# Row factors spread over partitions on TensorE, a longer allowance for transfers in the planner, and two staging buffers for output weights

## The chip, the cores and the metric

One core of a Trainium2 chip runs the kernel. The metric is the device time of one execution in microseconds (us), lower is better; the time of the kernel before is the median of three runs. A profile is one further execution with the hardware profiler on. The engines are called PE (TensorE), DVE (VectorE), ACT (ScalarE), POOL (GpSimd) and SP (SyncE, which issues all the DMAs of this kernel). Each engine runs its own list of instructions in order.

## What is computed

One encoder layer on a sequence of 4096 tokens with 1024 features, all float32 in and out:

```python
h = rmsnorm(x, pre_norm_g)
q, k, v, g_a, u_p, g_p = jnp.split(h @ w_in, splits, axis=-1)
a = banded_attention(q, k, v, rel_bias, sink) * jax.nn.silu(g_a)
p = multiscale_pool(u_p, pool_w, pool_scale) * jax.nn.silu(g_p)
mixed = jnp.concatenate([a, p], axis=-1) @ w_out
x = x + rmsnorm(mixed, post_norm_g)
```

`rmsnorm` multiplies each token by one number, its row factor: one over the root of the mean of the squares of its 1024 features. The attention looks 128 tokens to both sides; the pooling takes means over windows of 2, 4, 8 and 16 tokens.

## The kernel before, in words

Products are made of float16 pairs (a high part and the rest), three matmuls in place of one, and as blocks of 2 by 2 with seven products in place of eight. The program has two parts, one behind the other on every engine.

**Part A** (up to about 540 us) makes the three 512-wide projections: gate of the pooling `g_p` (GP), pooled values `u_p` (UU) and gate of the attention `g_a` (GA). The tokens come in 8 chunks of 512, `m` = 0 to 7. Chunk 0 is multiplied plainly (`plain`, tiles `plain`); chunks 1 to 7 have three `quad`s each, one for GP, UU and GA. A quad has seven products of 24 matmuls of 128x256 on the PSUM banks `y` (two of them, by turns), `x` and `v`. The first two, into `y` and `x`, read `xb`, the chunk's operands; the third reads `xt`, the sums of them; four of the seven read `xt`. Between the first and the third, ACT copies the bank (`keep`, line 718, `cc<-y`), since the third adds to it.

**What makes a chunk ready** is `prepare(m)`. Four times it loads 128 tokens into the one tile `xn` and ACT squares and sums them (`square`, line 324); POOL then takes the power, which leaves 512 row factors in `rs4`, token by partition (`root`). The operands, though, have features on partitions and tokens along the row, so the factors are needed along the row, the same in every partition. For that, SP stores `rs4` into memory (`rs_store`, line 907) and loads it back, spread over 128 partitions, into `rsb` (`rs_load`, line 910). For each of four slices `c`, DVE then multiplies the transposed tokens `nt` by gain and factor (`norm`, line 309, `nt<-nt,gsc,rsb`, two of 128x512), ACT makes the high parts of `xb` and DVE the rest, DVE makes the sums, and ACT and DVE split these into `xt`. For chunk 0 alone the factors are spread by PE already: DVE multiplies an identity by the factors of 128 tokens, a column of them at a time (`diag`), and a matmul of all ones with that diagonal leaves each factor in all partitions (`spread`, line 384).

**The order of part A comes from a planner** (`Steps`). Every step is given with its engine, an estimate of its time, a rank (`key`) and the names that it reads and writes. `run` plays the steps on five engines: the engine that is free soonest takes, of the steps whose inputs are ready by then, the one of the lowest rank. The order that comes out is the order of the program, fixed before it runs; on the chip, semaphores make each instruction wait for its data. A transfer is taken to move one after the other at the given length, and to be readable 1.8 us after its end:

```python
if dma:
    dma_free = max(dma_free, t + us) + dma
    end = dma_free + 1.8
```

SP's steps stand in one list too: a store that waits for its data holds every load behind it.

**Also in part A**: at chunk 0 `u_prod` multiplies the weights of UU by `pool_w` on PE, ACT squares the result and DVE copies it (`u_keep`, line 868). At chunks 1 to 3 the weights of q, k and v are split (`wb_steps`), and at chunks 5 and 6 those of the output (`wo_steps`): for each of four slices, four times `wo_keep` has ACT cast a weight tile into `RAW[:, 3]`, DVE make the rest beside it, and SP store both with two DMAs.

**Part B** (from line 1159 on) is the attention and the output projection. Its order is a list of its own, by written times; the change doesn't touch it.

Of the kernel before, what the change touches and what calls it, by code (L numbers as in the profile page):

```python
# [8 lines left out]
F32 = mybir.dt.float32  # L9
# [4 lines left out]
ALU = mybir.AluOpType  # L14
# [42 lines left out]
class Steps:  # L57
# [28 lines left out]
    def run(self):  # L86
        n_steps = len(self.steps)
        users = [[] for _ in range(n_steps)]
        open_deps = []
        for n, s in enumerate(self.steps):  # L90
            open_deps.append(len(s[5]))
            for d in s[5]:
                users[d].append(n)
        ready = [0.0] * n_steps
        begun = [None] * n_steps
        free = dict.fromkeys(("PE", "DVE", "ACT", "POOL", "SP"), 0.0)
        dma_free = 0.0
        waiting = {e: [] for e in free}
        for n in range(n_steps):
            if not open_deps[n]:  # L100
                waiting[self.steps[n][0]].append(n)
        left = n_steps
        while left:
            best = None
            for e, ns in waiting.items():
                if ns:
                    t = max(free[e], min(ready[n] for n in ns))
                    if best is None or t < best[0]:
                        best = (t, e)
# [12 lines left out]
            left -= 1  # L122
            for u in users[n]:
                ready[u] = max(ready[u], end)
                open_deps[u] -= 1
                if not open_deps[u]:
                    waiting[self.steps[u][0]].append(u)
        self.begun, self.end = begun, max(free.values())
        for n in sorted(range(n_steps), key=lambda n: (begun[n], n)):
            _, _, _, fn, args, _, _ = self.steps[n]  # L130
            fn(*args)
# [3 lines left out]
def hybrid_layer(ctx: ExitStack, tc, io, out):  # L135
# [41 lines left out]
    f_scr = dram.tile([NH, FR + 1, NF], F32, name="f_scr")  # L177
    rs_scr = dram.tile([NM, T], F32, name="rs_scr")
    x_scr = dram.tile([NU, P, 2, 2, 2, HK, P], F16, name="x_scr")
# [30 lines left out]
    with ExitStack() as actx:  # L210
# [18 lines left out]
        diags = [pa.tile([P, P], F32, name=f"diag{i}") for i in range(2)]  # L229
# [150 lines left out]
        def diag(i):  # L380
            t_scalar(V, diags[i // 2], ident, rs4[:, i : i + 1], ALU.mult)

        def spread(i):
            nc.tensor.matmul(
                bc[0][:, i * P : (i + 1) * P], onesf, diags[i // 2], start=True, stop=True,
                skip_group_check=True,
            )

# [74 lines left out]
        for h in range(2):  # L463
# [16 lines left out]
            for i in blocks:  # L480
                do("DVE", 0.25, -3, diag, i, r=["ident", f"rs{h}"], w=[f"diag{i // 2}"])
                do("PE", 0.5, -3, spread, i, r=["onesf", f"diag{i // 2}", "bc"], w=[f"bc{i}"])
            for c in range(HK):
# [216 lines left out]
        def quad(m, q, g):  # L700
# [48 lines left out]

            xbk_ = xkeys(m, "b")  # L750
            xtk = xkeys(m, "t")
            prod(0, yb, y, Y, A11, x_b(m, 0, 0), xbk_, True, False)
# [93 lines left out]

        ld(9, pw, io["pool_w"].rearrange("j p c -> p j c"), 0.25, w=["pw"])
        wut = flat32(XT0).rearrange("p (j c) -> p j c", j=4)
# [24 lines left out]
        for j in range(4):  # L873
            ld(9.5 + 0.1 * j, wut[:, j], io["w_uT"][j], 0.5, w=[f"wut{j}"])
            z = turn("sq")
            for half in range(2):
                t = U0 + 4 * j + 2 * half
                do("PE", 1.0, t, u_prod, j, half, r=["pw", f"wut{j}"], w=[f"wup{half}"] + bcs)
                do("ACT", act(512), t + 1.2, u_square, j, half, z, r=[f"wup{half}"], w=[f"sqt{z}"])
                do("DVE", dve(512), t + 1.2, u_keep, j, half, r=[f"sqt{z}"],  # L880
                   w=[f"wup{half}", f"tile{UU}.{j}{half}"])
            do("PE", 0.5, U0 + 4 * j + 5, w_norm, z, "u4", j, 4, b, r=["ones", f"sqt{z}"],
               w=[f"n2{b}"])
# [21 lines left out]

        def rs_store(m):
            nc.sync.dma_start(rs_scr[m].rearrange("(i p) -> p i", p=P), rs4)

        def rs_load(m):
            nc.sync.dma_start(  # L910
                rsb, rs_scr[m].rearrange("(o t) -> o t", o=1).to_broadcast([P, T])
            )

        def prepare(m):
            key = start(m) - 55
            b = m % 2
            for i in range(4):
# [3 lines left out]
               w=["rs4", "rs0", "rs1"])  # L921
            do("SP", 0.45, key + 4, rs_store, m, r=["rs4"], w=["rsd"], dma=0.1)
            do("SP", 0.45, key + 5, rs_load, m, r=["rsd"], w=["rsb", "pw"], dma=0.8)
            for c in range(HK):
# [4 lines left out]
                for h in range(2):  # L929
                    do("DVE", dve(512), k + h, norm, m, c, h, r=["gs", "rsb"], w=[n])  # L930
                x_operands(m, c, k + 2, "DVE")
# [34 lines left out]
        def row_prod():  # L966
            row_t["p"] = psa.tile([NH, 512], F32, name="fp", tag="wup0")
            nc.tensor.matmul(row_t["p"], row_t["b"], row_t["o"], start=True, stop=True)
# [14 lines left out]
        def row_steps(key):  # L983
            do("SP", 0.9, key, row_load, w=["row", "sqt0"], dma=0.3)
            do("PE", 1.8, key + 5, row_prod, r=["row", "sqt0"], w=["rowp", "wup0"])
            do("DVE", 0.7, key + 8, row_keep, r=["rowp", "wup0"], w=["rows", "sqt1"])
            do("SP", 0.45, key + 10, row_store, r=["rows", "sqt1"], w=["frow"], dma=0.1)
# [94 lines left out]

        stage16 = RAW[:, 3].bitcast(F16).rearrange("p (v c) -> p v c", v=2)

# [5 lines left out]

        def wo_store(k, o):
            for i in range(2):
                nc.sync.dma_start(w_scr[o + i, :, :, k, :], stage16[:, :, i * 512 : i * 512 + 512])

        def wo_keep(k, i, o, key):
            do("ACT", act(D), key, lambda: A.copy(stage16[:, 0], RAW[:, i]), r=[f"RAW{i}"],
               w=["RAW3"])
            do("DVE", dve(D), key + 1,
               lambda: tt(V, stage16[:, 1], RAW[:, i], stage16[:, 0], ALU.subtract),
               r=[f"RAW{i}"], w=["RAW3"])  # L1100
            do("SP", 0.9, key + 2, wo_store, k, o, r=["RAW3"], dma=1.8)

        def wo_steps(k, key):
# [5 lines left out]
            do("ACT", act(D), key + 1, wo_scale, 1, HK + k, r=["rowsc"], w=["RAW1"])  # L1109
            wo_keep(k, 0, O11, key + 2)  # L1110
# [4 lines left out]
            wo_keep(k, 1, O21, key + 8)  # L1115
            wo_keep(k, 2, OT1, key + 14)
# [4 lines left out]
            wo_keep(k, 0, OT4, key + 20)  # L1121

# [6 lines left out]
        for m in range(1, NM):  # L1129
# [820 lines left out]
```

## Time and profile before

| | |
|---|---|
| time, median of 3 runs | 1226.35 us (1225.23 to 1227.17) |
| the profiled execution | 1232.08 us; its span, first to last instruction, 1230.2 us |
| granted TensorE clock, mean | 0.991 |
| PE matmul busy | 1158.8 us, 94% |
| DVE, ACT, POOL busy | 952.0, 695.5 and 321.6 us (77%, 57%, 26%) |
| DMA moved | 227.92 MB |

In a row of the timeline stand the start and the duration in us, engine, line, operation and tiles (out<-in, with shapes), and the count of instructions that were joined; in brackets the time for which the engine had been idle before, and what ended that. Buffer numbers are left out: `y` is a bank of any quad. In the table by stretches stand, for each stretch, its length, then for PE, PEld (weight loads), DVE, ACT and POOL the busy time and the count, then the granted clock, the share of the DMA engines and GB/s. SPq is SP's list of DMAs; a row there is an issue, not the transfer.

### The profile page before, as it was taken

The page shows a single profiled execution, that of the slowest core. Times are in us where ns is not written, and L with a number is a line of the kernel's source. Part 1 is how long each engine was busy: PE and PEld are TensorE (multiplying, and loading weights), DVE is VectorE, ACT ScalarE, POOL GpSimd, SP SyncE. Part 2 cuts the span into 40 slices and gives each one's busy share as a digit, 9 for nine tenths or more (in the row PEclk, how much of TensorE's full clock was granted, in tenths as well). Part 3 has the DMA queues.
Part 4 walks back from the last instruction along what each step waited for, and adds up shares of the span by engine and source line. Part 5 has one row for each costly group of instructions (what it writes and reads, how often), then busy time and mean ns, then how long its engine had stood idle before and what let it go on. Part 6 is the DMA issues. An engine that isn't in the chain of part 4 may idle for free. (4 is left out here: it accounts for less than half of the span.)

```text
span 1230.2 us, 31539 instructions
## 1 busy us (share of the span) xinstructions
PE 1158.8 (94%) x13153; PEld 886.2 (72%) x13158; DVE 952.0 (77%) x1876; ACT 695.5 (57%) x1435; POOL 321.6 (26%) x310
## 2 busy tenths in 40 slices
PE   4995978999999999999999999999999999999997
PEld 4984867888888888886666776767676666767643
DVE  7868868797878978356778778777887887787786
ACT  5754545462635544236666756666576567566662
POOL 1002111112010202011254344434433533443331
PEclk9997998999999999999999999999999999999999
DMA  9635478966857555377989767866776786677694
GB/s 325 222 102 176 119 173 278 222 223 183 288 122 247 162 158 191 112 248 156 242 171 206 158 140 193 201 163 156 198 184 132 190 206 167 130 197 155 145 251 120
DMA packets 306848, 227.92 MB, mean 185 GB/s; under 512 B 205921, under 2 KB 269665, under 8 KB 302097
## 3 DMA queue, kind: packets, MB, share of 16 engines
q1 hardware_dynamic: 306704, 225.90, 69.9%
q8 instruction: 103, 1.69, 0.6%
q14 instruction: 41, 0.33, 0.1%
HBM read 116.78 MB, written 60.34 MB: 144 GB/s over the span
## 5 line engine op out<-in xcount | busy, mean ns | idle before, releaser
L604 PEld LDWEIGHTS <-wq 128*128 128x128 f16 x4104 | 404.3, 99 | 91.1 <-issue 34.3
L604 PE MATMUL y<-xt,wq 128*128 128x256 f16 x1512 | 179.2, 276 | 18.5 <-ACT cc L718 18.4
L1277 ACT ACTIVATE p<-p,nm 128x385 f32<-128x385 f32 (+1 forms) x256 | 153.0, 599 | 59.1 <-POOL p L1260 37.9
L1198 PE MATMUL aq<-xb,xb 128*128 128x256 f16 x1024 | 173.0, 273 | 4.5 <-DVE mo L1550 4.4
L1307 DVE SCALAR_TENSOR_TENSOR pn<-p,rd,pn 128x384 f16<-128x384 f32 (+1 forms) x256 | 156.5, 658 | 26.3 <-ACT pn L1299 26.3
L1522 PE MATMUL ms<-wo,ys 128*128 128x512 f16 x720 | 162.7, 379 | 1.8 <-ACT pn L1299 1.8
L1266 DVE CUSTOM_DVE_ANT_0 p<-s,nt,nsink 128x384 f32<-128x384 f32 (+1 forms) x256 | 156.0, 665 | 1.3 <-PE s L1243 1.1
L1299 ACT ACTIVATE pn<-p,rd 128x384 f16<-128x384 f32 (+1 forms) x256 | 136.3, 596 | 23.9 <-ACT p L1277 21.1
L1198 PEld LDWEIGHTS <-xb 128*128 128x128 f16 x1280 | 125.0, 98 | 22.8 <-issue 6.5
L1198 PE MATMUL aq<-xb,xt 128*128 128x256 f16 x512 | 139.5, 273 | 0.0
L1522 PEld LDWEIGHTS <-ys 128*128 128x128 f16 x720 | 69.0, 98 | 83.7 <-issue 3.0
L306 POOL TENSOR_TENSOR yt<-yt,sg 128x512 f32<-128x512 f32 (+2 forms) x32 | 50.7, 1586 | 290.6 <-DVE yt L309 246.6
L1522 PE MATMUL m<-wo,y 128*128 128x512 f16 x540 | 119.7, 379 | 1.4 <-POOL y L1427 0.7
L1522 PEld LDWEIGHTS <-y 128*128 128x128 f16 x540 | 51.4, 98 | 64.9 <-issue 3.6
L1556 POOL TENSOR_TENSOR mo<-mo,gpost 128x512 f32<-128x512 f32 x39 | 64.5, 1655 | 85.3 <-ACT jkb L1545 84.1
L1284 DVE TENSOR_SCALAR den<-den 128x4 f32<-128x4 f32 x64 | 17.4, 272 | 76.6 <-ACT p L1277 76.5
L604 PE MATMUL plain<-xb,wq 128*128 128x256 f16 x576 | 68.4, 277 | 5.3 <-ACT wq L537 2.5
L1388 PE MATMUL o<-pt,vv 128*64 128x256 f16 x1128 | 68.7, 274 | 3.6 <-DMA pt<-pn 3.6
L1198 PEld LDWEIGHTS <-xt 128*128 128x128 f16 x640 | 62.6, 98 | 12.6 <-issue 4.1
L604 PE MATMUL y<-xb,wq 128*128 128x256 f16 x504 | 60.7, 278 | 7.6 <-DVE ubuf L298 7.5
L1388 PEld LDWEIGHTS <-vv 128*64 128x64 f16 x1128 | 59.2, 110 | 10.4 <-issue 9.0
L1243 PE MATMUL s<-k_all,q 64*32 64x288 f16 (+7 forms) x3648 | 63.0, 266 | 3.1 <-ACT q L1186 1.4
(194 smaller groups left out, 1899.5 us busy)
## 6 DMA issues: line engine op xcount, KB each, us to landing
xn<-in_x SPq DMA_DIRECT2D x28, 512.0 KB, 3.9
nt<-in_xT SPq DMA_DIRECT2D x28, 512.0 KB, 5.3
x_scr<-xb SPq DMA_DIRECT2D x14, 1024.0 KB, 9.9
xb<-x_scr SPq DMA_DIRECT2D x14, 1024.0 KB, 7.8
xr<-in_x SPq DMA_DIRECT2D x28, 512.0 KB, 4.6
out<-xr SPq DMA_DIRECT2D x28, 512.0 KB, 3.7
ga_scr<-cc SPq DMA_DIRECT2D x64, 128.0 KB, 2.4
raw<-in_w_out SPq DMA_DIRECT2D x16, 512.0 KB, 8.0
```

What stands on the lines that cost most here:

```text
L306: eng.tensor_tensor(out=out, in0=in0, in1=in1, op=op)
L604: nc.tensor.matmul(b[:, s].rearrange("p (u t) -> p u t", u=2), wq[:, slot[q, op], wv, s, k, :], x[:, :, xv, k, :], start=(first and k + s ...
L1198: nc.tensor.matmul(a3, w[:, j, k, :], x[:, :, kh, v, kt, :], start=(n == 0), stop=(n == 3 * KT - 1),)
L1243: nc.tensor.matmul(s_ps[qs, gg, c0:c1], q_t[u, half][a, qi, jj, tl + 32 * hq : tl + 32 * hq + 32], k_all[a, ki, kc + c0 - s0 : kc + c1 - s ...
L1266: nc.vector.tensor_tensor_reduce(out=p_t[b, half][:, hh, :nk], in0=s_t[jj][:, gg, :nk], in1=bias[:, h, lo : lo + nk], scale=negc[:, h : h ...
L1277: nc.scalar.activation(p[:, hh, : nk + 1], p[:, hh, : nk + 1], AF.Exp, bias=nm_t[b, half][:, hh : hh + 1], scale=-1.0, accum_out=den_t[b, ...
L1284: nc.vector.tensor_scalar(out=den, in0=den, scalar1=1.0 / P_SCALE, scalar2=None, op0=ALU.mult)
L1299: nc.scalar.activation(prob_view(b, half)[:, 0, i], p_t[b, half][:, i, :nk], AF.Copy, scale=rd_t[b, half][:, i : i + 1],)
L1307: nc.vector.scalar_tensor_tensor(out=pn4[:, 1, i], in0=p_t[b, half][:, i, :nk], scalar=rd_t[b, half][:, i : i + 1], in1=pn4[:, 0, i], op0= ...
L1388: nc.tensor.matmul(o_ps[a, 2 * half : 2 * half + 2], v[:, vi, kt, a], pt[b, half][:, pi, g, :, i, :], start=(n == 0), stop=(n == last),)
L1522: nc.tensor.matmul(z_t[u, tag], y[:, k, yi, :], wo[o][:, wi, k, :], start=(n == 0 and acc is None), stop=(n == 3 * HK - 1), skip_group_che ...
L1556: eng.tensor_tensor(out=mo, in0=mo, in1=gpost[:, cs], op=ALU.mult)
```

## The change

1. **Row factors.** For chunks 1 to 7, DVE multiplies the identity by all 512 factors at once into a diagonal `dg` of 128 x 4 x 128 (`diag_all`), one matmul of 128x512 with the ones spreads them into a PSUM bank (`spread_all`), and `norm` reads that bank in place of `rsb`. The store and the load through memory go. The bank has a tag of the two that `u_prod` used (`wup0`, `wup1`), by turns; the small product of the bias rows moves from that tag to `n20`. `pool_w` now lies in the tile `ws`.
2. **Planner.** From 25 us on, what a transfer brings is readable 5.0 us after its end, not 1.8. So steps are put in another order on all engines; no transfer is changed by that itself.
3. **Planner, products.** Each product of a quad becomes four steps of six matmuls, each waiting only for its slice of the operands. The matmuls are the same, but the planner may now put pieces of two or three products in turn.
4. **`u_keep`** moves from DVE to ACT.
5. **Output weights.** `wo_keep` takes by turns `RAW[:, 3]` and the two square tiles `sq` as its stage, stores with four DMAs of half the size each, and the slices are ranked 24 apart, not 28.

```diff
-                end = dma_free + 1.8
+                end = dma_free + (1.8 if dma_free < 25.0 else 5.0)
...
-        rsb = pa.tile([P, T], F32, name="rsb")
-        pw = rsb.rearrange("p (j c) -> p j c", j=4)
+        dg = pa.tile([P, 4, P], F32, name="dg")
...
+        pw = ws[:, :T].rearrange("p (j c) -> p j c", j=4)
...
+        def diag_all():
+            tt(V, dg, ident.rearrange("p (o c) -> p o c", o=1).to_broadcast([P, 4, P]),
+               rs4.rearrange("p (i o) -> p i o", o=1).to_broadcast([P, 4, P]), ALU.mult)
+
+        def spread_all(m):
+            bc[m] = psa.tile([P, T], F32, name=f"bc{m}", tag=f"wup{m % 2}")
+            nc.tensor.matmul(
+                bc[m], onesf, dg.rearrange("p i c -> p (i c)"), start=True, stop=True
             )
...
-            stt(n, n, gsc[:, k : k + 1], rsb, ALU.mult, ALU.mult)
+            stt(n, n, gsc[:, k : k + 1], bc[m], ALU.mult, ALU.mult)
...
             def prod(slot, bk, tag, bkey, op, x, xk, first, last):
-                do("PE", SL, base + SL * slot, product, bk, tag, q, op, x, first, last,
-                   r=wkeys(q, op) + xk, w=[bkey])
+                for k in range(HK):
+                    do("PE", SL / 4, base + SL * (slot + 0.25 * k), product, bk, tag, q, op, x,
+                       first, last, range(k, k + 1),
+                       r=wkeys(q, op) + [f"{xk}.{k}{v}" for v in "hl"], w=[bkey])
...
-            V.tensor_copy(dst, n2_t.pop(("up", j, half)))
+            A.copy(dst, n2_t["up", j, half])
...
-            do("SP", 0.45, key + 4, rs_store, m, r=["rs4"], w=["rsd"], dma=0.1)
-            do("SP", 0.45, key + 5, rs_load, m, r=["rsd"], w=["rsb", "pw"], dma=0.8)
+            do("DVE", 0.75, key + 4, diag_all, r=["rs4", "ident"], w=["dg"] + [f"dg{i}" for i in range(4)])
+            do("PE", 1.0, key + 5, spread_all, m, r=["dg", "onesf"], w=[f"wup{m % 2}"])
...
-        stage16 = RAW[:, 3].bitcast(F16).rearrange("p (v c) -> p v c", v=2)
+        half3 = RAW[:, 3].bitcast(F16).rearrange("p (v c) -> p v c", v=2)
+        stages = [([half3[:, 0], half3[:, 1]], ["RAW3"]), ([t.bitcast(F16) for t in sqt], ["sqt0", "sqt1"])]
...
-        def wo_store(k, o):
+        def wo_store(k, o, stage):
             for i in range(2):
-                nc.sync.dma_start(w_scr[o + i, :, :, k, :], stage16[:, :, i * 512 : i * 512 + 512])
+                for v in range(2):
+                    nc.sync.dma_start(
+                        w_scr[o + i, :, v, k, :], stage[v][:, i * 512 : i * 512 + 512]
+                    )
...
-                    wo_steps(k, start(5) + 28 * k)
+                    wo_steps(k, start(5) + 24 * k)
```

The change moves instructions on every engine of part A. The planner, which orders them, plays the same rules with the new figures. Two places follow, at chunk 1, as the programs have them.

The list of ACT where the operands of chunk 1 are finished and its first quad runs, **before**. `xn,ssq1` is a square for chunk 3, `xb1` and `xt1` are the last slices of chunk 1's operands, and `cc4<-y0` is the copy of the bank between the quad's first and third product:

```order
L421 CAST xb1_68<-nt_69 128x2x4x128
L324 ACTIVATE xn_115,ssq1_119<-xn_115 128x1024
L441 CAST xt1_105<-nt_69 128x4x2x128
L324 ACTIVATE xn_115,ssq1_119<-xn_115 128x1024
L718 COPY cc4_129<-y0_1183 128x512
L537 ACTIVATE wq_107<-wq_107,sw_73 128x1024
L718 COPY cc0_125<-y0_1183 128x512
```

The same place **with the change**; here `xn,ssq0` is the last square for chunk 2 and `xn,ssq1` the first for chunk 3:

```order
L429 CAST xb1_68<-nt_69 128x2x4x128
L322 ACTIVATE xn_114,ssq0_117<-xn_114 128x1024
L449 CAST xt1_104<-nt_69 128x4x2x128
L728 COPY cc4_126<-y0_1163 128x512
L726 ACTIVATE cc2_124<-y1_1216,uf_77 128x512
L728 COPY cc0_122<-y0_1163 128x512
L545 ACTIVATE wq_106<-wq_106,sw_73 128x1024
L322 ACTIVATE xn_114,ssq1_118<-xn_114 128x1024
L728 COPY cc1_123<-y0_1163 128x512
```

Two squares stood between the last slice of `xb` and the copy; one does now, for the chunk before, and the squares for chunk 3 have moved behind the quad's second copy.

The list of DVE where chunk 1's factors are first used, **before** (`nt` are its tokens, `wq` weights that are being split):

```order
L309 SCALAR_TENSOR_TENSOR wq<-wq,com 128x1024
L306 TENSOR_TENSOR wq<-wq 128x1024
L309 SCALAR_TENSOR_TENSOR wq<-wq,sw 128x1024 x3
L309 SCALAR_TENSOR_TENSOR nt<-nt,gsc,rsb 128x512
L309 SCALAR_TENSOR_TENSOR wq<-wq,sw 128x1024
L309 SCALAR_TENSOR_TENSOR nt<-nt,gsc,rsb 128x512 x2
L306 TENSOR_TENSOR nt<-nt 128x512
```

The same place **with the change**:

```order
L307 SCALAR_TENSOR_TENSOR wq<-wq,com 128x1024 x2
L307 SCALAR_TENSOR_TENSOR wq<-wq,sw 128x1024 x3
L304 TENSOR_TENSOR raw<-raw 128x1024
L304 TENSOR_TENSOR dg<-ident,rs_112 128x512
L307 SCALAR_TENSOR_TENSOR wq<-wq,sw 128x1024
L307 SCALAR_TENSOR_TENSOR wq<-raw,sw,wq 128x1024
L307 SCALAR_TENSOR_TENSOR nt<-nt,gsc,bc_930 128x512 x4
L304 TENSOR_TENSOR nt<-nt 128x512
```

The diagonal is made one step ahead of where the first `norm` stood, two splits of weights lie between it and the first `norm`, and four `norm`s now follow in one go.

On PE the matmul that spreads chunk 1's factors, `bc<-dg,onesf` (line 393 of the changed kernel), stands behind 396 of the 576 matmuls of chunk 0. The first product of 24 matmuls is no longer in one piece: six of `x`, `y` or `v` take turns, so 666 matmuls of 128x256 precede the first one that reads `xt` of chunk 1, where there were 624.

More of the change, by code (lines that the diff above doesn't have):

```diff
@@ L480, in hybrid_layer @@
             for i in blocks:
-                do("DVE", 0.25, -3, diag, i, r=["ident", f"rs{h}"], w=[f"diag{i // 2}"])
-                do("PE", 0.5, -3, spread, i, r=["onesf", f"diag{i // 2}", "bc"], w=[f"bc{i}"])
+                do("DVE", 0.25, -3, diag, i, r=["ident", f"rs{h}"], w=[f"dg{i}"])
+                do("PE", 0.5, -3, spread, i, r=["onesf", f"dg{i}", "bc"], w=[f"bc{i}"])
             for c in range(HK):
@@ L877, in hybrid_layer @@
                 t = U0 + 4 * j + 2 * half
-                do("PE", 1.0, t, u_prod, j, half, r=["pw", f"wut{j}"], w=[f"wup{half}"] + bcs)
+                do("PE", 1.0, t, u_prod, j, half, r=["ws", f"wut{j}"], w=[f"wup{half}"] + bcs)
                 do("ACT", act(512), t + 1.2, u_square, j, half, z, r=[f"wup{half}"], w=[f"sqt{z}"])
-                do("DVE", dve(512), t + 1.2, u_keep, j, half, r=[f"sqt{z}"],
-                   w=[f"wup{half}", f"tile{UU}.{j}{half}"])
+                do("ACT", act(512), t + 1.2, u_keep, j, half, r=[f"wup{half}"],
+                   w=[f"tile{UU}.{j}{half}"])
             do("PE", 0.5, U0 + 4 * j + 5, w_norm, z, "u4", j, 4, b, r=["ones", f"sqt{z}"],
@@ L904, in hybrid_layer @@
         sum_weights(GA, sw[:, 4:5], "a4", M1 + 27, 3.0, "DVE")
[L906 to L912, printed above, removed]
         def prepare(m):
@@ L929, in prepare @@
                 for h in range(2):
-                    do("DVE", dve(512), k + h, norm, m, c, h, r=["gs", "rsb"], w=[n])
+                    do("DVE", dve(512), k + h, norm, m, c, h, r=["gs", f"wup{m % 2}"], w=[n])
                 x_operands(m, c, k + 2, "DVE")
@@ L1089, in minus, with wo_keep @@
             tt(V, o, a, b, ALU.subtract)
-        def wo_store(k, o):
+        def wo_store(k, o, stage):
             for i in range(2):
[L1093 to L1101, printed above, removed]
+                for v in range(2):
+                    nc.sync.dma_start(
+                        w_scr[o + i, :, v, k, :], stage[v][:, i * 512 : i * 512 + 512]
+                    )
+        def wo_keep(k, i, o, key, n):
+            stage, sk = stages[n % 2]
+            do("ACT", act(D), key, lambda: A.copy(stage[0], RAW[:, i]), r=[f"RAW{i}"], w=sk)
+            do("DVE", dve(D), key + 1, lambda: tt(V, stage[1], RAW[:, i], stage[0], ALU.subtract),
+               r=[f"RAW{i}"], w=sk)
+            do("SP", 1.8, key + 2, wo_store, k, o, stage, r=sk, dma=1.8)
         def wo_steps(k, key):
@@ L1120, in wo_steps @@
                w=["RAW0"])
-            wo_keep(k, 0, OT4, key + 20)
+            wo_keep(k, 0, OT4, key + 20, 3)
         def wb_load(j):
```

23 lines of the change are left out of this document (10 added, 13 removed).

## The prediction

> **What bounds the kernel now.** I read the table by stretches first, to see where PE has room, then PE's timeline, then the lists of the engines that end its waits. The chain of waits that ended last lies wholly in part B (it starts at 1177.81 us), which the change leaves alone, so it doesn't help here.
>
> ```profile
> 0.00:96.66 96.66, 80.39 (x744) 71.99 (x745) 71.02 (x130) 59.21 (x78) 5.15 (x11) 1.00 0.65 211
> 96.66:200.00 103.34, 76.23 (x644) 65.07 (x643) 84.32 (x126) 47.65 (x66) 19.39 (x14) 0.90 0.66 186
> 200.00:330.00 130.00, 124.40 (x1139) 109.93 (x1139) 107.47 (x193) 70.50 (x96) 17.26 (x14) 1.00 0.76 220
> 330.00:540.00 210.00, 208.25 (x1918) 185.73 (x1920) 154.56 (x224) 88.81 (x113) 26.32 (x18) 1.00 0.56 170
> 540.00:1230.20 690.20, 669.52 (x8715) 453.50 (x8712) 534.60 (x1205) 429.36 (x1084) 253.49 (x253) 1.00 0.75 179
> ```
>
> The first figure after the length is PE's busy time. The first row is chunk 0 with its start, the last is part B. PE is busy nearly throughout but in the second row: there it stands idle for 103.34 - 76.23 = 27.11 us, and the granted clock was 0.90. In the third and fourth it is idle for 5.60 and 1.75 us, so for 34.46 us in all from 96.66 to the end of part A.
>
> ```profile
> 64.40 32.26 PE L604 MATMUL plain<-xb,wq 128*128 128x256 f16 x294
> 104.11 5.17 PE L604 MATMUL y<-xb,wq 128*128 128x256 f16 x24 [7.45 <-DVE ubuf L298]
> 118.54 4.59 PE L604 MATMUL y<-xt,wq 128*128 128x256 f16 x24 [6.65 <-ACT cc L718]
> 176.45 2.78 PE L604 MATMUL y<-xb,wq 128*128 128x256 f16 x24
> 179.07 2.78 PE L604 MATMUL x<-xb,wq 128*128 128x256 f16 x24
> 189.80 4.80 PE L604 MATMUL y<-xt,wq 128*128 128x256 f16 x24 [7.95 <-ACT cc L718]
> 304.54 2.78 PE L604 MATMUL v<-xb,wq 128*128 128x256 f16 x24 [2.74 <-DVE cc L306]
> ```
>
> Three waits make up 22.05 us of it. Each also slows what comes next: the 24 matmuls behind them took 5.17, 4.59 and 4.80 us where others took 2.78, together 6.22 us; behind the wait of 2.74 us they didn't. The Trainium skill (TensorE: Matmul & The Clock Gate, HAM oscillation) says that gaps of over some 3.4 us put PE back to half clock, and the trace agrees; worked out as 3.4 us at half speed three times, it would make the slow spells an estimated 5.1 us, and the gain below 1.1 us smaller.
>
> **Why PE waits.** The first wait is for a DVE that had lost time on the way of the factors through memory:
>
> ```profile
> 64.28 1.04 POOL L306 TENSOR_TENSOR rs<-ssq,mhalf 128x4 f32<-128x4 f32 x1
> 65.35 0.36 SPq L907 DMA_DIRECT2D rs_scr<-rs  x1
> 77.27 0.33 SPq L910 DMA_DIRECT2D rsb<-rs_scr  x1
> 81.92 0.75 DVE L309 SCALAR_TENSOR_TENSOR nt<-nt,gsc,rsb 128x512 f32<-128x512 f32 x1 [9.49 <-DMA rsb<-rs_scr]
> 103.19 0.87 DVE L298 TENSOR_SCALAR ubuf<-plain,uf 128x256 f32<-128x256 f32 x2
> SPq L910 <- DMA rs_scr<-rs: 8.6, 1, 8.6
> ```
>
> The factors were there at 65.3, and first used at 81.92: DVE stood still for 9.49 us, and the emptying of a bank that PE needed at 96.66 came at 103.19. The last row is from SP's own waits: it stood 8.6 us for the store, with all later loads behind it. The other two waits are for ACT, which was held by a square ahead of the copy:
>
> ```profile
> 116.87 1.06 ACT L324 ACTIVATE xn<-xn 128x1024 f32<-128x1024 f32 x1 [8.30 <-DMA xn<-in_x]
> 117.93 0.56 ACT L718 COPY cc<-y 128x512 f32<-128x512 f32 x1
> 175.03 0.38 SPq L131 DMA_DIRECT2D xn<-in_x  x1
> 176.51 6.45 SPq L935 DMA_DIRECT2D x_scr<-xb  x2
> 187.38 1.06 ACT L324 ACTIVATE xn<-xn 128x1024 f32<-128x1024 f32 x1 [10.37 <-DMA xn<-in_x]
> 189.18 0.56 ACT L718 COPY cc<-y 128x512 f32<-128x512 f32 x1
> DMA to landing us min/median/max: 3.4/3.9/10.5
> ```
>
> That square is not needed for a whole chunk. The planner put it there because it took its load (512 KB) to be readable 0.5 / 0.3 + 1.8 = 3.5 us after its issue; the median was 3.9 and the longest 10.5.
>
> **Spread on PE: what it costs.**
>
> ```profile
> 23.06 0.73 PE L384 MATMUL bc<-diag,onesf 128*128 128x128 f32 x4
> 23.62 0.60 PE L604 MATMUL plain<-xb,wq 128*128 128x256 f16 x4
> 44.81 1.06 PE L856 MATMUL wup<-rsb,xt 128*128 128x128 f32 x8
> 45.70 0.82 PE L604 MATMUL plain<-xb,wq 128*128 128x256 f16 x6
> L309 DVE SCALAR_TENSOR_TENSOR nt<-nt,gsc,rsb 128x512 f32<-128x512 f32 x56 | 41.1, 745 | 26.1 <-DMA nt<-in_xT 15.9 <-DMA rsb<-rs_scr 10.0
> L1396 DVE SCALAR_TENSOR_TENSOR at<-o,gaf,gb 128x512 f32<-128x512 f32 x32 | 23.8, 742 | 1.2 <-PE o L1388 1.2
> L306 DVE TENSOR_TENSOR cc<-x,cc 128x512 f32<-128x512 f32 x14 | 9.6, 684 | 4.0 <-ACT cc L718 2.7 <-PE x L604 1.2
> ```
>
> No row is a float32 matmul of 128x512. Four of 128x128 took PE from 44.81 to 45.70, 0.89 us; two of `bc` took 0.56, so four would take 1.12. I take 0.89, the longer run of the two, so 7 x 0.89 = **6.2 us** (7.8 by the other row), all of it on the path, since PE is the bound. It can't be nothing: PE has no idle time for it if the waits go. The diagonal is one DVE step of 128x512, 0.68 us by the row of `cc`; DVE isn't the bound over a chunk. `norm` now reads a bank: a DVE step of the same kind with one operand from a bank took 742 ns, against 745, so nothing. Two DMAs a chunk leave SP, and with them its 8.6 us of standing. The spread is a new wait in PE's list: if a diagonal is late, all the matmuls behind it are.
>
> **What comes after the waits: chunk 1.** PE had done all 576 matmuls of chunk 0 at 96.66 and 282 of them at 64.40, at 32.26 / 294 = 0.110 us each, so it comes to the spread, behind 396, at 76.9.
>
> ```profile
> 67.15 4.25 ACT L537 ACTIVATE wq<-wq,sw 128x1024 f16<-128x1024 f32 x4
> 107.41 1.22 DVE L306 TENSOR_TENSOR xb<-nt,xb 128x1024 f16<-128x1024 f32 x1
> 108.54 0.70 DVE L306 TENSOR_TENSOR ws<-ubuf 128x527 f32<-128x527 f32 x1
> 113.95 0.69 DVE L309 SCALAR_TENSOR_TENSOR yt<-ws,ubuf 128x512 f32<-128x512 f32 x1
> 107.41:175.03 67.62, 58.73 (x78) 0.94 0.58 171
> ```
>
> With the change the last square stands behind three of those four weight steps: done by 71.5, the factors 1.4 us later (64.28 to 65.3 and an addition ahead of it), the diagonal by some 74.5, 2.4 us ahead of PE. So `norm` starts at 76.9 + 0.9 = 77.8, 4.1 us sooner than before. From there to the last slice of `xb` DVE took 108.63 - 81.92 = 26.7 us. In the new list there stand between them two pooling tiles more (108.54 to 114.64 without one `xt` step of 1.22: 4.9 us) and, on balance, two weight steps of 128x1024 less (1.2 us each, like the row of 107.41): 29.2 us, so 107.0. PE asks for that slice after 72 matmuls of chunk 1, at 96.66 + 0.9 + 72 x 0.109 = 105.4. It waits some 2 us; I take **3** for the chunk, in place of 7.45 + 6.65 and 4.20 of slow matmuls.
>
> **Chunk 2.** Between the last `xb` slices of chunks 1 and 2 DVE was busy for 58.7 of 67.6 us. Less the two pooling tiles, plus a diagonal: 54.5, so 107.0 + 54.5 = 161.5. PE comes to that slice 426 matmuls later (2.62 us for 24, by the starts at 176.45 and 179.07: 46.5), with two spreads and a norm of weights 2.4: 155.9. So a wait of 5.6 and something for DVE's own: **7 us**, in pieces, in place of 27.11 - 14.10 = 13.01 and 2.02 of slow matmuls.
>
> **Chunks 3 to 7.** 7.35 us of waits now; the longest is the 2.74 above. The longer allowance should take some, the new order will bring others: **7.35** stay.
>
> **The rest.** `u_keep`: eight copies of 128x512, 0.6 us each by the copies `cc<-y`, go to ACT, which was busy for 59.21 of 96.66 us there: 4.5 us into 37 of room, so nothing; without that room they would be late for the weights of UU by as much. The two stages:
>
> ```profile
> 406.20 1.18 SPq L1093 DMA_DIRECT2D w_scr<-raw  x2
> ACT raw L1096 <- DMA w_scr<-raw: 13.2, 5, 5.4
> ```
>
> The second row is ACT's wait for the stage to be stored: 13.2 us that go, but off PE's path, which is 99% busy there. The first gives 0.6 us an issue: 32 issues more are 19 us of SP's list over chunks 5 to 7. I take nothing; a load of `nt` right behind four of them is 2.4 us late at worst, and DVE has a quarter of its time free to cover it. Near the end of part A DVE now waits for the mask of the bias rows, whose load stands behind the last stores, and two steps that empty banks for PE stand behind that. Its bound is a landing, 3.9 us; I take nothing, since PE's list has products on the other banks ahead of those.
>
> **Sum.** Gone: 27.11 + 6.22. Comes: 6.2 + 3 + 7. Gain 33.3 - 16.2 = 17.1 us; the profiled execution's 1232.08 would be 1215.0. It ran 0.5% over the median, which I take over as it is: 1226.35 - 17.1 = **1209.3**, between some 1200 and 1218 with the doubtful terms.
>
> **The rivals.** A measurement of this kernel can tell 0.2%, 2.45 us, from no change.
>
> - *No wait is left*: 34.46 + 6.22 - 6.2 = 34.5 us, so 1191.9. For it: chunks 3 to 7 nearly are so. Against: DVE's arithmetic above.
> - *The allowance doesn't catch the late loads*, so the change does half of what it says: the load of 187.38 took 12 us because 2 MB of `x_scr` went out beside it, and 1.7 + 5.0 = 6.7 us doesn't cover that. Both waits for ACT stay with their slow spells, 6.65 + 1.81 + 7.95 + 2.02 = 18.4, in place of the 7 of chunk 2: gain 5.7, so 1220.6. For: the new order still has a square between two copies of a quad. Against: that load is now issued before the stores. The Trainium skill (DMA: Bandwidth & Descriptors, Anatomy of one DMA) gives 2.0 us and bytes over 436 GB/s, an estimated 3.2 us here; by that the old allowance was right and the new one only delays. The median of 3.9 is near to it, the 10.5 is not.
> - *Slower: DVE becomes the bound in every chunk.* The pieces of products in turn let PE ask for a chunk sooner, and the factors wait for PE's list; if `xb` comes late by the 6.65 + 1.81 us of the wait at 118.54 in each of six chunks, that is 50.8 us in place of 40.7 - 6.2 = 34.5: 1242.6. It decides from 34.5 / 6 = 5.7 us a chunk. For: DVE was 82% busy to 200. Against: 74% from 330 to 540, with PE 99% busy.
> - *No change that can be told* would need part of this: the waits for ACT stay, and 5 us of new ones.
>
> **How the numbers follow.** Forecast 0.58, no wait left 0.10, late loads 0.14, no change 0.05, slower 0.13. So faster 0.82, same 0.05, slower 0.13. The range from 1196 to 1227 holds the forecast's cases, the late loads, about 0.04 of the first rival and most of no change: 0.8.
>
> **What would show it.** Rows of `nt<-nt,gsc,bc` that start near 78; the first `y<-xt` of chunk 1 with a wait under 3 us, and matmuls of 2.78 us behind it; the spread's row at 0.9 us; no square with 8 us of waiting ahead of a `cc<-y`. Wrong would be: a spread of over 1.1 us, PE idle for over 17 us between 97 and 200, or new waits of over 12 us behind 200.

## The result and the profile after

The changed kernel took 1205.62 us (median of 4 runs, 1204.73 to 1208.5) beside 1226.76 for the kernel before on the same chip: 0.983 of it, 95% interval 0.981 to 0.985. With a later group of runs it was 1204.52 beside 1232.39, 0.979 (0.976 to 0.982). The kernel before moved by 5.6 us between the groups and the changed one by 1.1, so below each kernel is given as a ratio to the runs of before in its own group. The forecast was 1209.3, faster.

The table by stretches of the changed kernel, columns as in the prediction; part A now ends with the last product at 506.66 us instead of 533.72:

```profile
96.66:200.00 103.34, 98.06 (x894) 86.42 (x893) 99.08 (x155) 60.40 (x81) 15.28 (x13) 1.00 0.59 199
200.00:330.00 130.00, 130.00 (x1170) 113.11 (x1169) 100.54 (x188) 68.69 (x94) 19.04 (x16) 1.00 0.70 236
330.00:506.66 176.66, 175.68 (x1606) 156.33 (x1604) 136.79 (x195) 74.52 (x96) 20.95 (x16) 1.00 0.52 164
506.66:1206.70 700.04, 678.28 (x8782) 460.54 (x8779) 536.38 (x1208) 431.34 (x1087) 254.12 (x253) 0.99 0.75 179
```

PE's idle time behind 96.66 us fell from 34.46 to 5.28 + 0 + 0.98 us, and the clock in the first row is 1.00, not 0.90. These are all the waits that are left in PE's timeline, with two of the spreads and what follows each:

```profile
77.84 1.10 PE L393 MATMUL bc<-dg,onesf 128*128 128x512 f32 x2
78.77 3.44 PE L612 MATMUL plain<-xb,wq 128*128 128x256 f16 x30
109.35 0.60 PE L612 MATMUL y<-xb,wq 128*128 128x256 f16 x4 [2.68 <-DVE xb L304]
113.03 0.82 PE L612 MATMUL x<-xb,wq 128*128 128x256 f16 x6 [0.47 <-DVE cc L304]
115.65 1.02 PE L393 MATMUL bc<-dg,onesf 128*128 128x512 f32 x2
116.51 0.82 PE L612 MATMUL v<-xt,wq 128*128 128x256 f16 x6
121.93 2.13 PE L612 MATMUL y<-xt,wq 128*128 128x256 f16 x18 [0.67 <-ACT cc L728]
125.51 0.81 PE L612 MATMUL v<-xb,wq 128*128 128x256 f16 x6 [1.45 <-DVE cc L304]
343.03 0.81 PE L612 MATMUL v<-xt,wq 128*128 128x256 f16 x6 [0.98 <-DVE cc L304]
```

The spreads take 0.93 and 0.86 us from their start to the next matmul. DVE's list shows the walk through chunk 1, and the group of ACT's squares the other half:

```profile
77.00 0.69 DVE L304 TENSOR_TENSOR dg<-ident,rs 128x512 f32<-128x512 f32 x1 [1.24 <-POOL rs L304]
80.00 2.72 DVE L307 SCALAR_TENSOR_TENSOR nt<-nt,gsc,bc 128x512 f32<-128x512 f32 x4
108.07 1.22 DVE L304 TENSOR_TENSOR xb<-nt,xb 128x1024 f16<-128x1024 f32 x1
L322 ACT ACTIVATE xn<-xn 128x1024 f32<-128x1024 f32 x22 | 23.1, 1052 | 0.3 <-DMA xn<-in_x 0.3
```

The same group of the kernel before (from 96 to 330 us in both), where the figures behind the second bar are ACT's idle time ahead of the squares and what ended it:

```profile
L324 ACT ACTIVATE xn<-xn 128x1024 f32<-128x1024 f32 x21 | 22.1, 1054 | 46.2 <-DMA xn<-in_x 46.1
```

46.1 us of ACT's waiting for loads became 0.3. So far it looks as forecast. The experiments show that the longer allowance, which I named for this, does end ACT's waits, but that the time was gained by another part of the change.

### The profile page after: what moved, and what is told of

It reads as the page before. It is cut to its first block, busy times and chain, and to the rows that moved or that the text cites. A ratio compares the mean times of both kernels' runs of the same rounds, so it can differ in the third digit from the quotient of the medians.

```text
span 1206.7 us, 31584 instructions
## 1 busy us (share of the span) xinstructions
PE 1161.5 (96%) x13172; PEld 886.8 (73%) x13172; DVE 947.6 (79%) x1875; ACT 699.1 (58%) x1443; POOL 318.1 (26%) x310
## 5 line engine op out<-in xcount | busy, mean ns | idle before, releaser
L612 PE MATMUL y<-xt,wq 128*128 128x256 f16 x1512 | 203.2, 273 | 0.7 <-ACT cc L728 0.7
L1281 ACT ACTIVATE p<-p,nm 128x385 f32<-128x385 f32 (+1 forms) x256 | 153.0, 599 | 58.1 <-POOL p L1264 37.9
L304 POOL TENSOR_TENSOR yt<-yt,sg 128x512 f32<-128x512 f32 (+2 forms) x32 | 46.9, 1465 | 309.0 <-DVE yt L307 307.3
L612 PE MATMUL y<-xb,wq 128*128 128x256 f16 x504 | 68.8, 273 | 2.7 <-DVE xb L304 2.7
L612 PE MATMUL v<-xb,wq 128*128 128x256 f16 x504 | 68.3, 273 | 1.5 <-DVE cc L304 1.5
L612 PE MATMUL v<-xt,wq 128*128 128x256 f16 x504 | 68.6, 273 | 1.0 <-DVE cc L304 1.0
```

The costliest lines, as they stand in the source:

```text
L304: eng.tensor_tensor(out=out, in0=in0, in1=in1, op=op)
L612: nc.tensor.matmul(b[:, s].rearrange("p (u t) -> p u t", u=2), wq[:, slot[q, op], wv, s, k, :], x[:, :, xv, k, :], start=(first and k + s ...
L1281: nc.scalar.activation(p[:, hh, : nk + 1], p[:, hh, : nk + 1], AF.Exp, bias=nm_t[b, half][:, hh : hh + 1], scale=-1.0, accum_out=den_t[b, ...
```

## The experiments

Four groups of runs. "ACT" is ACT's idle time ahead of squares for loads of `xn` from 96 to 330 us; "PE" the sum of PE's waits in part A behind 96.66 us. Both are from one profiled execution of each kernel.

| kernel | us | ratio to before (95%) | ACT | PE |
|---|---|---|---|---|
| changed kernel, first group | 1205.62 | 0.983 (0.981 to 0.985) | 0.3 | 6.3 |
| before (three later groups) | 1232.1 to 1232.4 | 1 | 46.1 | 34.0 |
| allowance alone | 1224.70 | 0.995 (0.993 to 0.997) | 2.5 | 21.8 |
| spread alone | 1202.47 | 0.977 (0.975 to 0.979) | 9.3 | 4.7 |
| pieces alone | 1226.20 | 0.996 (0.994 to 0.998) | 37.9 | 26.1 |
| all but the spread | 1224.31 | 0.995 (0.994 to 0.997) | 3.2 | 26.3 |
| spread, and an unread store | 1219.63 | 0.991 (0.988 to 0.994) | 26.6 | 15.3 |
| before, packets of 16 bytes | 1209.70 | 0.983 (0.981 to 0.986) | 14.8 | 15.1 |
| changed kernel again | 1204.52 | 0.979 (0.976 to 0.982) | 0.9 | 5.0 |
| spread and allowance | 1215.17 | 0.987 (0.985 to 0.990) | 1.2 | 11.2 |
| changed, old allowance | 1202.69 | 0.976 (0.972 to 0.980) | 11.5 | 4.7 |
| changed, whole products | 1208.83 | 0.980 (0.976 to 0.985) | 1.9 | 9.0 |
| spread and pieces | 1207.94 | 0.980 (0.976 to 0.984) | 7.9 | 8.4 |
| changed, each spread three times | 1212.99 | 0.984 (0.980 to 0.988) | 1.9 | 3.4 |

**The allowance alone** (in the kernel before).

```
-                end = dma_free + 1.8
+                end = dma_free + (1.8 if dma_free < 25.0 else 5.0)
```

> The kernel before with the allowance of 5.0 us alone. Theory (the two waits for ACT come from squares planned ahead of their loads): the waits of 6.65 and 7.95 us go with their slow matmuls, 18.4 us, the first wait for DVE (7.45) stays: 1226.8 - 18.4 = 1208, and no square waits 8 us ahead of a copy. Rival 1 (the loads are late by the stores of x_scr, which no allowance of 5 us covers): 1226 within 2.5 us, both waits still there. Rival 2 (what an engine is spared comes back at the next wait, since DVE is behind by then): the waits for ACT go, but waits for DVE of about the same sum stand in their place, 1220 to 1229.

The squares no longer wait, but PE does, for slices of chunk 1 that come late:

```profile
108.32 0.59 PE L604 MATMUL y<-xb,wq 128*128 128x256 f16 x2 [4.85 <-ACT xb L421]
114.17 1.01 PE L604 MATMUL y<-xb,wq 128*128 128x256 f16 x4 [5.26 <-DVE xb L306]
123.29 1.01 PE L604 MATMUL y<-xb,wq 128*128 128x256 f16 x4 [5.00 <-DVE xb L306]
L324 ACT ACTIVATE xn<-xn 128x1024 f32<-128x1024 f32 x21 | 22.1, 1052 | 2.6 <-DMA xn<-in_x 2.5
```

Rival 2 holds: the longer allowance does what it says for ACT, and the time comes back as waits for DVE's and ACT's slices. The gain is 0.5%, not 18 us. (The trace is of the shortest of the six runs, 1218.58 us, so its waits may be shorter than those of the median.)

**The spread alone** (allowance, whole products, one stage and the copy as before; norm reads the bank).

```
-            do("SP", 0.45, key + 4, rs_store, m, r=["rs4"], w=["rsd"], dma=0.1)
-            do("SP", 0.45, key + 5, rs_load, m, r=["rsd"], w=["rsb", "pw"], dma=0.8)
+            do("DVE", 0.75, key + 4, diag_all, r=["rs4", "ident"], w=["dg"] + [f"dg{i}" for i in range(4)])
+            do("PE", 1.0, key + 5, spread_all, m, r=["dg", "onesf"], w=[f"wup{m % 2}"])
```

> The kernel before with the spread on TensorE alone (memory round trip gone, old allowance, whole products, one stage). Theory (the first wait is for a DVE that waited for the factors): the wait of 7.45 us and its 2.4 us of slow matmuls go, seven spreads of 0.86 us come, 6.0 us: gain 3.8, 1223. Rival (the spread moves the late point: DVE sooner, but the waits for ACT grow by what PE comes sooner): nothing gone, 6.0 us come, 1233.

Both sides of this were far off: it gained 29.9 us, as much as the whole change or a little more. The norm of chunk 1 starts at 70.72 instead of 81.92, and the two long waits for ACT are gone with the old allowance still in place:

```profile
70.72 0.74 DVE L308 SCALAR_TENSOR_TENSOR nt<-nt,gsc,bc 128x512 f32<-128x512 f32 x1
100.02 1.22 DVE L305 TENSOR_TENSOR xb<-nt,xb 128x1024 f16<-128x1024 f32 x1
L323 ACT ACTIVATE xn<-xn 128x1024 f32<-128x1024 f32 x20 | 21.1, 1054 | 9.5 <-DMA xn<-in_x 9.3
```

**The pieces alone.**

```
-                do("PE", SL, base + SL * slot, product, bk, tag, q, op, x, first, last,
-                   r=wkeys(q, op) + xk, w=[bkey])
+                for k in range(HK):
+                    do("PE", SL / 4, base + SL * (slot + 0.25 * k), product, bk, tag, q, op, x,
+                       first, last, range(k, k + 1),
+                       r=wkeys(q, op) + [f"{xk}.{k}{v}" for v in "hl"], w=[bkey])
```

> The kernel before with the products cut into four pieces alone. Theory (the cut gives PE nothing of its own: a piece waits for the same bank, copy and slice): 1226.8 within 4 us, the three long waits still there, none shorter by over 3 us. Rival (pieces of other products fill the waits, and most of the gain is theirs): the three waits are together under 10 us of 22, time 1213 or less.

0.4% faster. Waits of 5.54 and 5.40 us stay where 7.45 and 7.95 were; the one of 6.65 became 1.12, which the theory had excluded, but 2.79 and 2.20 came behind it. The sum went from 34.0 to 26.1: the pieces are not where the gain is from.

**All but the spread** (the changed kernel with the row factors through memory again).

```
-            do("DVE", 0.75, key + 4, diag_all, r=["rs4", "ident"], w=["dg"] + [f"dg{i}" for i in range(4)])
-            do("PE", 1.0, key + 5, spread_all, m, r=["dg", "onesf"], w=[f"wup{m % 2}"])
+            do("SP", 0.45, key + 4, rs_store, m, r=["rs4"], w=["rsd"], dma=0.1)
+            do("SP", 0.45, key + 5, rs_load, m, r=["rsd"], w=["rsb"] + [f"dg{i}" for i in range(4)], dma=0.8)
```

> The kernel after with the row factors through memory as before, all else as changed. Theory (the spread pays for itself in chunk 1 only): DVE waits for the factors at chunk 1 again, the wait of some 7.5 us and 2.4 us of slow matmuls come back, seven spreads of 0.86 us go: 1205.6 + 3.8 = 1209.5. Rival 1 (the longer allowance makes the planner start the round trip in time): no such wait, 1205.6 - 6.0 = 1199.6, so the spread costs. Rival 2 (with the round trip SP stands 8 us in each chunk, and loads behind it are late in all of them): waits in several chunks, over 1214.

My theory, that the spread pays in chunk 1 only, falls: without it 0.5% is left of the gain. The time is that of rival 2, and SP stood 26.1 us for the stores, in four waits. But the loads were not seen to be late in all chunks: ACT waited 3.2 us for them, and 20.1 of PE's 26.3 us of waits lie ahead of 133 us. DVE waited 4.45 us there for the factors, first used at 94.50, and PE for slices:

```profile
114.52 0.59 PE L614 MATMUL y<-xb,wq 128*128 128x256 f16 x2 [5.49 <-ACT xb L431]
118.28 1.01 PE L614 MATMUL y<-xb,wq 128*128 128x256 f16 x4 [3.18 <-DVE xb L306]
132.15 1.01 PE L614 MATMUL y<-xb,wq 128*128 128x256 f16 x4 [5.67 <-DVE xb L306]
```

Why should two small DMAs in a chunk do so much? In the kernel before, the loads that ACT waited for at 116.87 and 187.38 were issued at 106.28 and 175.03. Each stands some 2 us behind a store of row factors (issued at 104.19 and 173.10). The first of these, 2 KB, took 10.1 us to land; of the second the trace shows no landing. Such a store writes 512 numbers of 4 bytes, each by itself, since those of a partition lie 512 bytes apart in memory. In the stretches behind the two stores the DMA engines of the kernel before moved little, with loads of 512 KB outstanding (the last two columns are the DMA share and GB/s):

```profile
107.00:115.00 8.00, 4.75 (x36) 3.62 (x34) 7.79 (x12) 1.05 (x1) 2.44 (x2) 0.90 0.17 37
176.00:186.00 10.00, 5.85 (x54) 5.10 (x53) 1.12 (x3) 1.00 (x2) 0.00 (x0) 1.00 0.68 50
```

This gave a new theory, and the next two kernels test it.

**An unread store** beside the spread: nobody reads it or waits for it but the next writer of the four numbers.

```
+            do("SP", 0.45, key + 4, rs_store, m, r=["rs4"], w=["rsd"], dma=0.1)
             do("PE", 1.0, key + 5, spread_all, m, r=["dg", "onesf"], w=[f"wup{m % 2}"])
```

> The spread alone, with the old store of the row factors to memory beside it, which nobody reads or waits for. Spread alone was 0.977 of before. Theory (that store is 512 packets of 4 bytes and keeps the DMA queue for 8 to 10 us, in which the loads behind it don't move): the stretches of 8 us at under 60 GB/s behind it come back, loads of xn behind it land after 10 us instead of 4, and at least 10 of the 29 us that the spread brought are lost, 0.985 or more. Rival 1 (SP stood for the store's end before the second DMA, and that made the loads late): this store is waited for by nobody, so 0.977 within 0.002. Rival 2 (the order of the lists was lucky): no low stretches behind the stores, and a time between.

The store alone takes 17 of the 29.9 us back. Behind its store of 244.69:

```profile
246.00:256.00 10.00, 6.34 (x59) 5.53 (x57) 5.20 (x9) 1.34 (x2) 0.00 (x0) 1.00 0.98 51
256.93 1.06 ACT L323 ACTIVATE xn<-xn 128x1024 f32<-128x1024 f32 x1 [9.59 <-DMA xn<-in_x]
258.20 0.75 DVE L308 SCALAR_TENSOR_TENSOR nt<-nt,gsc,bc 128x512 f32<-128x512 f32 x1 [6.90 <-DMA nt<-in_xT]
258.71 5.10 PE L613 MATMUL y<-xt,wq 128*128 128x256 f16 x24 [6.36 <-ACT cc L725]
```

The DMA engines are busy 98% of that stretch and move 51 GB/s; ACT, DVE and PE all wait for it in turn. "Busy" means here that packets stand: of the 115 packets of 4096 bytes that start in this stretch, 33 took over 2 us and the longest 8.77, where the median from 60 to 400 us is 159 ns. The 512 packets of the store, which start by 247.01, are themselves put down with some 9 ns each. The theory holds in that the loads behind the store are late, though in the two stretches of the kernel before the DMA engines were not all that busy (0.17 and 0.68), and what they waited for the trace doesn't show. SP's standing for the store's end (rival 1) isn't needed for the late loads. But SP also stood 11.3 us, in seven waits, for the factors that these stores carry, with the loads behind it, and part of the 17 us may be that. In the next kernel all engines' lists are those of the kernel before, so it is free of this doubt.

**Packets of 16 bytes** in the kernel before: the four factors of a partition lie side by side in memory.

```
-            nc.sync.dma_start(rs_scr[m].rearrange("(i p) -> p i", p=P), rs4)
+            nc.sync.dma_start(rs_scr[m].rearrange("(p i) -> p i", p=P), rs4)
...
+            rv = rsb.rearrange("p (q i) -> p i q", i=4)
```

> The kernel before, round trip through memory kept, but the store writes the four factors of a partition side by side: 128 packets of 16 bytes instead of 512 of 4 bytes; DVE reads them in the other order. Theory (the 512 packets hold the queue): the store is done in about a quarter of its 10 us, the low stretches shrink to some 3 us, the waits of 7.45, 6.65 and 7.95 us are together under 10 us, and the time is under 0.988 of before, if the strided reading of the factors costs DVE nothing. Rival (a round trip of two DMAs in a row is long whatever the packets): DVE still waits for the factors, 0.995 to 1.000.

The layout of one store gave 0.983, as much as the whole change in its first group. PE's longest wait is 2.94 us now, where three of over 6 us stood. SP stood for the store 2.2 us at most (8.6 before), and a stretch behind a store now moved 334 GB/s:

```profile
205.00:213.00 8.00, 8.00 (x79) 7.21 (x78) 6.23 (x15) 3.47 (x6) 0.00 (x0) 1.00 0.96 334
L309 DVE SCALAR_TENSOR_TENSOR nt<-nt,gsc,rsb 128x512 f32<-128x512 f32 x56 | 63.7, 1151 | 11.7 <-DMA nt<-in_xT 10.1 <-DMA rsb<-rs_scr 1.6
SPq L911 <- DMA rs_scr<-rs: 2.9, 2, 2.2
```

The second row is a likely reason why it isn't faster still: read in steps of four numbers, the factors make a norm step 1151 ns long instead of 745, 22.7 us more for DVE over 56 steps, and 13.3 of PE's 15.1 us of waits end with DVE. A kernel with such packets and factors that DVE reads side by side was not run.

The counts of packets, of this kernel and of the one before, show what was changed: 2689 packets fewer, where seven stores with 128 packets in place of 512 make 2688.

```profile
DMA packets 304159, 227.92 MB, mean 189 GB/s; under 512 B 203232, under 2 KB 266976, under 8 KB 299408
DMA packets 306848, 227.92 MB, mean 185 GB/s; under 512 B 205921, under 2 KB 269665, under 8 KB 302097
```

The Trainium skill (DMA: Bandwidth & Descriptors, Rules for kernel authors) says that a last dimension that isn't contiguous becomes one descriptor per element, and to rearrange it. The counts agree. That rule gives no price; the unread store cost 17 us here. For the step of 1151 ns the Trainium skill (SBUF — State Buffer, Door 1: The DMA port swizzle) has lines of 16 bytes, with a penalty where each access comes to a new one. The factors here do just that, and the row agrees.

The traces also keep each packet's time, and this parts all the kernels. Packets of 512 bytes and more that started from 60 to 400 us and took over 2 us: 117 in the kernel before, 78 with the allowance alone, 126 with the pieces alone, 87 in all but the spread, and 147 beside the unread store. These are the five kernels with the 4-byte stores. In the nine other profiled executions, this kernel's and those of the experiments below among them, there is a single one, of 2.08 us.

**The changed kernel again, and spread with allowance** (the diff of the allowance as above).

> The changed kernel once more beside the others of this group. If the spread alone is really faster than the whole change, it is 0.981 to 0.985 of before here too; else near 0.977.

0.979, with an interval that leaves open whether the spread alone is faster.

> The spread and the allowance of 5.0 us, whole products and one stage. Theory (with the stores gone the loads come in 4 to 5 us, so the longer allowance has nothing left to cover): 0.977 of before within 0.002, like the spread alone. Rival 1 (the allowance is what makes the whole change slower than the spread alone, by putting DVE's and ACT's work later): 0.981 to 0.985. Rival 2 (it takes the 4.7 us of waits that the spread alone has left): 0.974 or less.

Rival 1: on the spread with whole products, the allowance costs 12.7 us against the spread alone. The norm starts 9 us later (70.72 there): the planner puts the squares of chunk 1 later, the last at 72.25 instead of 62.90, and POOL starts on the factors at 75.51 instead of 64.44. The last slice of chunk 1 comes at 114.16 instead of 101.24:

```profile
79.58 2.72 DVE L308 SCALAR_TENSOR_TENSOR nt<-nt,gsc,bc 128x512 f32<-128x512 f32 x4
112.94 1.22 DVE L305 TENSOR_TENSOR xb<-nt,xb 128x1024 f16<-128x1024 f32 x1
114.21 1.01 PE L613 MATMUL y<-xb,wq 128*128 128x256 f16 x4 [5.00 <-DVE xb L305]
```

**The changed kernel with the old allowance** (that line back to 1.8).

> The changed kernel with the old allowance of 1.8 us. The prediction's step (the longer allowance is what takes the two waits for ACT away): they come back, 14.6 us and 3.8 us of slow matmuls, 1223. Theory now (the stores' end did that; the allowance only shifts the lists): no square waits over 3 us ahead of a copy, 0.977 to 0.981 of before, the same as the whole change or a little less.

1202.69: the two waits for ACT don't come back. One square still waited 4.57 us ahead of a copy (at 226.96), which the theory had excluded, but no wait of PE followed. The longer allowance was not needed for the time, though ACT waits 11.5 us for loads without it.

**The changed kernel with whole products.**

> The changed kernel with whole products. The spread with the allowance alone was 0.987 of before, with waits of 3.7, 2.5 and 5.0 us for late slices of xb in chunk 1; the whole change 0.979. Theory (the cut into pieces lets PE go on with other products while a slice is late, so the allowance does no harm): without the cut those waits are there again, 0.985 to 0.989. Rival (the two stages or the moved copy made the difference): 0.979 within 0.002.

The waits are there again, though smaller (0.91, 2.93 and 4.21 us). But the ratio of 0.980 is the rival's, and its interval just reaches the theory's 0.985. The median is 4.3 us over that of the changed kernel in the group before, and 6.3 us under that of spread and allowance there, which lacks the two stages and the moved copy. So the pieces and those two may each be worth a few us here; this isn't shown.

**Spread and pieces**, without the two stages, the moved copy and the allowance.

> The spread and the cut into pieces, old allowance, one stage, the copy on DVE. Theory (after the spread nothing is left but some 5 us of waits in chunks 1 and 2, and the two stages and the moved copy are off PE's path): 0.975 to 0.979, like the spread alone and like the changed kernel with the old allowance. Rival (two stages and the moved copy are worth something): slower than the changed kernel with the old allowance by over 0.003.

5.2 us slower than the changed kernel with the old allowance in the same group (1207.61 to 1209.12 beside 1201.81 to 1206.86), with 8.4 us of PE's waits instead of 4.7; 2.3 of them lie from 404 to 506 us, where the output weights are made. So the two stages and the moved copy were worth something beside the pieces. Which of the two, and why the spread alone does as well without either, stays open.

**Each spread three times.**

```
+            for _ in range(3):
                 nc.tensor.matmul(
```

> The changed kernel with each spread done three times into the same bank (the result is the same). Theory (PE is the bound and its list is full, so each spread costs its row, 0.86 us): 14 more spreads, 12.0 us, 1216.5, 0.989 of before. Rival (a spread fills time that PE would wait in): under 4 us, 0.982 or less.

```profile
78.42 2.81 PE L394 MATMUL bc<-dg,onesf 128*128 128x512 f32 x6
81.08 2.13 PE L613 MATMUL plain<-xb,wq 128*128 128x256 f16 x18
```

Three take 2.66 us, 0.89 each. The last product of part A starts 10.5 us later than in the changed kernel's second run (514.86 beside 504.32): 14 x 0.89 = 12.4, less 1.7 us of waits that they fill. So in the traces a spread is paid in full, or nearly. The medians say less: 8.5 us between two groups, and a ratio of 0.984 that lies between theory and rival.

## Why the prediction was right, and where it wasn't

The time, the sign and the sum's form held; one cause did not, and two terms were too large. That the time came so near is luck in part. The changed kernel gained 21.1 us in the first group and 27.9 in the second, where 17.1 were forecast, and the waits that the sum gave to two parts of the change go with one of them alone, the spread.

- **Why PE waits, first wait: right, but only half.** DVE was held by the way through memory, and without the spread it is again. But the long part of that way is the store's 512 packets: with packets of 16 bytes, DVE waits 1.6 us for the factors in all, 10.0 before.
- **Why PE waits, the squares: wrong in the reason.** "The planner put it there because it took its load to be readable 3.5 us after its issue; the median was 3.9 and the longest 10.5." The allowance alone does end ACT's waits, as the step says, but gives the time back in chunk 1. And the long landings were no property of the loads: with the 4-byte stores gone, the old allowance leaves 9.3 of the 46.1 us and no long wait of PE. The rival "late loads" named the 2 MB of `x_scr` beside the load of 187.38; beside the unread store ACT waited until 256.93 for a load issued at 245.16, with no store of `x_scr` near it, so the 512 packets ahead of a load are enough. I had quoted SP's 8.6 us for a store of 2 KB and not asked why it took that long. The estimate of 3.2 us that the prediction took from the Trainium skill (DMA: Bandwidth & Descriptors, Anatomy of one DMA) spoke against a longer allowance. That section has it for transfers that GpSimd issues; here SP issues them, and the median was 3.9. The runs agree on the allowance, since with the spread the old one does as well.
- **Spread: right.** 0.89 forecast, 0.86 to 0.93 in the rows, 0.89 in the threefold run; a step that reads the bank took 739 ns, so nothing, as forecast.
- **Chunk 1: right in its walk.** The diagonal at 77.69 (forecast 74.5), just ahead of the spread at 77.84 and not 2.4 us, the norm at 80.00 (77.8, two weight steps stood ahead of it), the last slice at 109.29 (107.0). The wait for that slice was 2.68 us, and three smaller ones made 5.27 in all (3 forecast).
- **Chunk 2: too large.** 7 us forecast, none came. DVE had the slice at 160.88 (161.5 forecast), but PE, which had waited 5.27 us in chunk 1 and not 3 and had pieces of other products ahead of it, came to it at 160.93 and not at 155.9.
- **Chunks 3 to 7: too large.** 7.35 us were to stay, 0.98 did. The spread alone leaves none behind 155 us either, so they went with the way through memory too.
- **The rest, "I take nothing": not quite.** The stages and the copy were worth some 5 us in one pair of kernels.

The waits were 10 + 7.35 us in the forecast and 5.27 + 0.98 in the trace, 11.1 less, so part A should have gained 17.1 + 11.1 = 28.2 us; it gained 533.72 - 506.66 = 27.1. Part B, which isn't changed, took 700.04 us in this execution and 696.48 in that of before; in the spread alone it took 697.26. Part of the 3.6 us is a wait of 2.45 us for the last `pt` transfer, and slow matmuls behind it, where before had 1.08.

## What to carry to other kernels

A small transfer can cost more than a large one: look at how many packets it makes and at what is queued behind it, not at its bytes. Where a load is late, look for what was issued just ahead of it before giving it more time: more time in a planner moves all the work behind it. And a change of several parts that comes out as forecast says little on which of them did it.

## What the runs showed of the hardware

- A store of 2 KB in 512 packets of 4 bytes took 10.1 us to land, and 512 KB loads issued 2 us behind such stores landed after over 10 us where the median was 3.9. Single packets of 4096 bytes behind them took up to 8.77 us, against 159 ns in the median. In 128 packets of 16 bytes SP's wait for the store was 2.2 us instead of 8.6, and five of the six stores whose landing shows took 1.4 to 4.8 us. The sixth took 9.9, of which over 6 us went by before its first packet started.
- Slow matmuls don't follow the length of PE's wait alone: behind 2.94 and 2.37 us of waiting 24 matmuls took 4.19 and 4.45 us, behind 2.74 us in the kernel before 2.78. The granted clock was 0.64 from 148.20 to 152.40 us and 0.62 from 453.00 to 457.50. So gaps shorter than the 3.4 us that the prediction names can do it. PE's timeline of the kernel with packets of 16 bytes:

```profile
148.19 4.19 PE L605 MATMUL v<-xt,wq 128*128 128x256 f16 x24 [2.94 <-DVE ubuf L309]
452.96 4.45 PE L605 MATMUL v<-xb,wq 128*128 128x256 f16 x24 [2.37 <-DVE cc L306]
```
